# The down-projection of a feed-forward layer in seven products: the sum product moved to third place

## The chip, the cores and the metric

One of the eight cores of a Trainium2 chip runs the kernel. The metric is device time in microseconds (us) from one launch; lower is better. A core has TensorE (PE, matrix multiply, results in PSUM), VectorE (DVE), ScalarE (ACT), GpSimd (POOL) and SyncE (SP, which here issues DMA transfers). PEld is TensorE's loading of the stationary operand.

## The reference

A decoder layer on 1024 tokens of width 1024: a mixing part (pooling and differential attention), then a gated feed-forward part with 2816 channels. The change lies in the last matrix product of it:

```python
    h = rms_norm(x, norm_ffn_g[l], NORM_EPS)
    gu = h @ ffn_w_in[l].astype(h.dtype)
    g = causal_depthwise_conv(gu[..., :D_FF], ffn_conv_w[l], ffn_conv_b[l])
    u = gu[..., D_FF:]
    x = x + (jax.nn.silu(g) * u) @ ffn_w_out[l].astype(h.dtype)
return rms_norm(x, norm_final_g, NORM_EPS)
```

`ffn_w_out` is 2816 x 1024; all data are float32.

## The kernel before

Each float32 operand is split into a rounded high part (ScalarE, L85) and a remainder (L86: `lo = src - hi`, on VectorE or GpSimd); a product is then three matmuls, high by high, high by low and low by high (`mm3`, L148 to L151).

The down-projection (L730 to L864) doesn't compute its four output quarters with eight block products but with seven, in the Strassen-Winograd way. The contraction over 2816 channels is cut into two halves of 11 tiles (channel tiles with even and with odd number), the 1024 output columns into two halves of 512, the tokens into two halves of four tiles. The activations' seven left operands are written to DRAM by the up-projection (`act_d`, rows "1" to "7"; `store_act`, L704; the last sums of them are lines L716 to L719). The weight has four quarters: x (first channel half, first column half), y (first, second), z (second, first) and v (second, second). Each takes three of the 14 buffers of the pool `h2` and comes in six transfers (`load_quarter`, L742). Three of the seven right operands are quarters as loaded, and four are differences, made in place by "updates" on VectorE (L757), in the order in which `DOWN` (L30) names them: x becomes y - x, later x becomes v - x; y becomes v - y; z becomes x - z.

One product runs over six steps (`STEPS`: five of two channel tiles, one of one). For a step, `operands` (L752) issues the update if there is one, loads the activations' rows (`ra`, two buffers) on SyncE's queue, splits them into `ah` (ScalarE) and `al` (VectorE), and splits the weight: high part on ScalarE, remainder on GpSimd. Steps 2, 4 and 6 put the weight's two parts into one `h2` buffer (named `b`), the other three into `bh` and `bl`; buffer tag "st" of `bh` and "sm" of `bl` are also used by sums of the up-projection. `tile_part` (L783) then does the step's matmuls for four token tiles, each into its own PSUM bank (`banks`, L777: products in even places take two "tp" banks, one "mm" and the "pv" bank; those in odd places three "sc" and one "mm"). After its last step a product's banks are added to the residual rows `xr` (`add_product`, L789; one addition of 128 x 512 per token tile and output quarter). `ADDS` (L32) says which quarters: (h, c) is token half h and column half c. Product 1 is wanted in all four quarters and product 6, too, in three of them. Together there are 56 additions (4 of them are the subtractions of product 4, L793).

The order before is 1, 2, 5, 7, 6, 3, 4. After the last product's steps 1 to 3, the final norm of the first four token tiles is done, then steps 4 to 6 and the norm of the others (`held`, `right_half`, `finish`).

The order in which each engine gets its instructions is not that of the code: the framework schedules all of them when the kernel is built, on a timeline of its own, and chooses a free buffer of a tag there. An engine then works its list off in that order and waits at an instruction whose inputs aren't there.

Of the kernel before, what the change touches and what calls it, by code (L numbers as in the profile page):

```python
# [22 lines left out]
NCT = FF // P  # L23
# [3 lines left out]
LAM_INIT = 0.8 - 0.6 * math.exp(-0.3 * 0)  # L27
NEG = -1e30
TW = 384
DOWN = (("1", "x", None), ("2", "z", None), ("5", "x", "yx"), ("7", "y", "vy"), ("6", "x", "vx"), ("3", "v", None),  # L30
        ("4", "z", "xz"))
ADDS = {"1": ((0, 0), (0, 1), (1, 0), (1, 1)), "2": ((0, 0),), "3": ((0, 1),), "4": ((1, 0),), "5": ((0, 1), (1, 1)),  # L32
        "6": ((0, 1), (1, 0), (1, 1)), "7": ((1, 0), (1, 1))}
STEPS = ((0, 2), (2, 2), (4, 2), (6, 2), (8, 2), (10, 1))
SCRATCH = 2048
# [13 lines left out]
def trunk_kernel(ctx, tc, x, norm_mix_g, w_in, pool_w, rows, line, rel_bias, w_out, norm_ffn_g,  # L49
                 ffn_w_in, ffn_w_out, norm_final_g, onehot, out):  # L50
    nc = tc.nc
    x, out, w_in, w_out = x[0], out[0], w_in[0], w_out[0]
# [18 lines left out]
    def sc_ps(name):  # L71
        return ps_a.tile([P, 512], F32, tag="sc", bufs=3, name=name)

    def pv_ps(name):
        return ps_a.tile([P, 512], F32, tag="pv", bufs=1, name=name)

    def tp_ps(name):
        return ps_a.tile([P, 4, P], F32, tag="tp", bufs=2, name=name)

    def mm_ps(name):  # L80
        return ps_a.tile([P, 512], F32, tag="mm", bufs=2, name=name)
# [63 lines left out]
                nc.tensor.transpose(tp[:, k, :], xn[:, (4 * q + k) * P:(4 * q + k + 1) * P], ident)  # L145
            psplit(hi[q][:, :, t * P:(t + 1) * P], lo[q][:, :, t * P:(t + 1) * P], tp)

    def mm3(ps, wh, wl, hh, hl, first, last):  # L148
        nc.tensor.matmul(ps, wh, hh, start=first, stop=False)  # L149
        nc.tensor.matmul(ps, wh, hl, start=False, stop=False)  # L150
        nc.tensor.matmul(ps, wl, hh, start=False, stop=last)  # L151


    nc.scalar.preload_act_table_set("natural_log_exp_and_others")
# [117 lines left out]
    def proj_half(ps, wh, wl, half):  # L272
        cs = slice(half * 512, half * 512 + 512)
        for k in range(KC):
            mm3(ps, wh[:, k, :], wl[:, k, :], hTh[k // 4][:, k % 4, cs], hTl[k // 4][:, k % 4, cs],
                k == 0, k == KC - 1)
# [456 lines left out]
    def load_x1_back():  # L733
        for t in range(NT):
            xt = u_tile(F32, f"xr_{t}")
            nc.vector.tensor_copy(xt[:, 0:1], last_w)
            nc.sync.dma_start(xt, x1_d[t * P:(t + 1) * P, :])
            xr.append(xt)
# [3 lines left out]
    def load_quarter(q):  # L742
        b, cs = dict(x=(0, 0), y=(0, 1), z=(1, 0), v=(1, 1))[q]
        src = ffn_w_out.rearrange("(m b p) c -> b p m c", b=2, p=P)[b][:, :, cs * 512:cs * 512 + 512]
        wq[q] = [h2.tile([P, 4, 512], F32, tag="h2", name=f"w{q}{i}") for i in range(3)]
        for m, n in STEPS:
            nc.sync.dma_start(wq[q][m // 4][:, m % 4:m % 4 + n, :], src[:, m:m + n, :])
# [4 lines left out]
    def operands(gi, m, n):  # L752
        num, q, upd = DOWN[gi]
        if upd:
            a, b = upd
            if q == b:
                nc.vector.tensor_tensor(quarter(b, m, n), quarter(a, m, n), quarter(b, m, n), op=ALU.subtract)  # L757
        raw = mid.tile([P, 2, 512], F32, tag="rw", bufs=2, name=f"ra{num}_{m}")[:, 0:n, :]
        nc.sync.dma_start(raw, op_rows(int(num), m, n))
        if gi == 0:  # L760
            a2 = h2.tile([P, 4, 512], F32R, tag="h2", name=f"a{num}_{m}")
            ah, al = a2[:, 0:n, :], a2[:, 2:2 + n, :]
        else:
            ah = wide.tile([P, 2, 512], F32R, tag="x", bufs=4, name=f"ah{num}_{m}")[:, 0:n, :]
            al = mid.tile([P, 2, 512], F32R, tag="cv", bufs=3, name=f"al{num}_{m}")[:, 0:n, :]
        split(ah, al, raw, nc.vector)
        if m // 2 % 2:
            b2 = h2.tile([P, 4, 512], F32R, tag="h2", name=f"b{num}_{m}")
            wh, wl = b2[:, 0:n, :], b2[:, 2:2 + n, :]
        else:  # L770
            wh = mid.tile([P, 2, 512], F32R, tag="st", bufs=2, name=f"bh{num}_{m}")[:, 0:n, :]
            pool, tag, bufs = (mid, "sm", 2) if gi else (wide, "x", 4)
            wl = pool.tile([P, 2, 512], F32R, tag=tag, bufs=bufs, name=f"bl{num}_{m}")[:, 0:n, :]
        split(wh, wl, quarter(q, m, n))
        return ah, al, wh, wl

    def banks(gi):  # L777
        if gi % 2:
            return [sc_ps(f"fo_{gi}_{j}") for j in range(3)] + [mm_ps(f"fo_{gi}_3")]
        return ([tp_ps(f"fo_{gi}_{j}").rearrange("p a b -> p (a b)") for j in range(2)]  # L780
                + [mm_ps(f"fo_{gi}_2"), pv_ps(f"fo_{gi}_3")])

    def tile_part(ps, op, j, m, n):  # L783
        ah, al, wh, wl = op
        js = slice(j * P, (j + 1) * P)
        for i in range(n):
            mm3(ps, ah[:, i, js], al[:, i, js], wh[:, i, :], wl[:, i, :], m + i == 0, m + i == NCT // 2 - 1)

    def add_product(num, j, ps):  # L789
        for h, c in ADDS[num]:  # L790
            t, cs = 4 * h + j, slice(c * 512, c * 512 + 512)
            if num == "4":
                nc.vector.tensor_tensor(xr[t][:, cs], xr[t][:, cs], ps, op=ALU.subtract)  # L793
            else:
                nc.vector.tensor_tensor(xr[t][:, cs], xr[t][:, cs], ps, op=ALU.add)  # L795
# [3 lines left out]
    def half_sum(t, half):  # L799
        if t not in outs:  # L800
            outs[t] = h2.tile([P, 4, 512], F32, tag="h2", name=f"o_{t}").rearrange("p a c -> p (a c)")[:, 0:D]
            sums[t] = small.tile([P, 2], F32, tag="fs", bufs=8, name=f"ss2_{t}")
        nc.scalar.activation(outs[t][:, 0:512], xr[t][:, half * 512:half * 512 + 512], AF.Square,
                             accum_out=sums[t][:, half:half + 1])

    def finish(t):
        o, ss = outs[t], sums[t]
        var = small.tile([P, 1], F32, tag="var", name=f"varl_{t}")
        nc.vector.tensor_scalar(var, ss[:, 0:1], 1.0 / D, ss[:, 1:2], op0=ALU.mult, op1=ALU.add)
        sd = small.tile([P, 1], F32, tag="lg", name=f"sd_{t}")  # L810
        nc.scalar.activation(sd, var, AF.Sqrt)
        r = small.tile([P, 1], F32, tag="rs", name=f"rsl_{t}")
        nc.vector.reciprocal(r, sd)
        r = newton(r, var, f"l{t}")
        nc.scalar.mul(o[:, 512:1024], o[:, 512:1024], r)
        nc.vector.scalar_tensor_tensor(o[:, 0:512], xr[t][:, 0:512], r, g_bc3[:, 0:512], op0=ALU.mult, op1=ALU.mult)
        if t < NT - 1:
            nc.sync.dma_start(out[t * P:(t + 1) * P, :], o)
            return
        nc.scalar.dma_start(out[t * P:(t + 1) * P, 512:1024], o[:, 512:1024])  # L820
        nc.sync.dma_start(out[t * P:(t + 1) * P, 0:512], o[:, 0:512])

    def right_half(t):
        half_sum(t, 1)
        nc.vector.tensor_scalar(sums[t][:, 1:2], sums[t][:, 1:2], 1.0 / D, EPS, op0=ALU.mult, op1=ALU.add)
        nc.gpsimd.tensor_tensor(outs[t][:, 512:1024], xr[t][:, 512:1024], g_bc3[:, 512:1024], op=ALU.mult)

    last_w = w_now["3"][0][:, 0, 0:1].bitcast(F32)
    late = 3
    for gi, (num, q, upd) in enumerate(DOWN):  # L830
        for c in (q if upd is None else upd):
            if c not in wq:
                load_quarter(c)
        if gi == 4:
            g_bc3 = mid.tile([P, D], F32, tag="gt", bufs=1, name="g_fin")
            nc.sync.dma_start(g_bc3, norm_final_g.unsqueeze(0).to_broadcast((P, D)))
        ps = banks(gi)
        last = gi == len(DOWN) - 1
        held = []
        for si, (m, n) in enumerate(STEPS):  # L840
            op = operands(gi, m, n)
            if last and si >= late:
                held.append((op, m, n))
                continue
            for j in range(4):
                tile_part(ps[j], op, j, m, n)
            if gi == 0 and si == 3:
                load_x1_back()
        if gi == 2:
            warm = small.tile([P, 1], F32, tag="warm", bufs=1, name="warm")  # L850
            nc.scalar.activation(warm, xr[0][:, 0:1], AF.Sqrt, bias=1.0, scale=0.0)
        if last:
            for t in range(NT):
                right_half(t)
            for t in range(4):
                half_sum(t, 0)
                finish(t)
        for j in range(4):
            for op, m, n in held:
                tile_part(ps[j], op, j, m, n)  # L860
            add_product(num, j, ps[j])
            if last:
                half_sum(4 + j, 0)
                finish(4 + j)  # L864
# [55 lines left out]
```

## Time and profile before

| | us |
|---|---|
| median of 3 runs | 1087.63 |
| the 3 runs | 1083.22, 1087.63, 1090.09 |
| profiled execution, its own time | 1088.16 |
| profiled execution, span from first to last instruction | 1086.3 |

The mean granted clock of TensorE in the span is 0.986 of full speed. The profile is one execution. Its times start with the span. Instructions of one engine can overlap a little at their ends, and the ends of matmuls are modelled, so the distance from start to start says what one costs. Idle time of an engine that nothing waits for costs nothing. The down-projection's matmuls begin at 856 us, between the last ones of the up-projection, and end at 1078.8 us. From 864.4 us on there are no others.

### The profile page before, as it was taken

How to read it: one execution, taken by the hardware profiler on the slowest of the kernel's cores; microseconds unless marked ns; L12 is line 12 of the kernel's file. 1: busy time of each engine (PE TensorE's matmuls, PEld its weight loads, DVE VectorE, ACT ScalarE, POOL GpSimd, SP SyncE). 2: the span in 40 equal slices, each digit the busy share in tenths (PEclk: the TensorE clock that was granted, in tenths of full speed). 3: DMA queues.
4: the chain of work that ended last, by engine and by line, in shares of the span. 5: the costliest groups of instructions: out<-in, count | busy, mean ns of one | idle time of the engine just before them, and what ended most of it. 6: DMA issues, size and time to landing. Idle time of an engine off the chain costs nothing. (4 is left out here: it accounts for less than half of the span.)

```text
span 1086.3 us, 13526 instructions
## 1 busy us (share of the span) xinstructions
PE 1034.2 (95%) x4879; PEld 859.7 (79%) x4879; DVE 746.2 (69%) x1192; ACT 513.5 (47%) x827; POOL 452.5 (42%) x304
## 2 busy tenths in 40 slices
PE   5999999999799998899999999999999998999997
PEld 4988888888677776778888888888888887788885
DVE  7556777868587579766775566567555678977646
ACT  5557467665763345434343344334343443345363
POOL 3232232433631235425444362444434455299342
PEclk9999999999899999999999999999999998999999
DMA  7111111101367753232322333232334784533333
GB/s 236 41 39 40 44 28 39 38 27 46 116 214 235 231 193 117 80 95 87 126 90 92 129 108 97 88 126 93 97 120 157 291 284 166 171 113 89 106 107 155
DMA packets 103686, 129.06 MB, mean 119 GB/s; under 512 B 4802, under 2 KB 67487, under 8 KB 103620
## 3 DMA queue, kind: packets, MB, share of 16 engines
q1 hardware_dynamic: 95268, 106.71, 30.8%
q10 hardware_dynamic: 8352, 21.50, 5.1%
q8 instruction: 38, 0.62, 0.2%
q14 instruction: 28, 0.23, 0.1%
HBM read 91.22 MB, written 36.97 MB: 118 GB/s over the span
## 5 line engine op out<-in xcount | busy, mean ns | idle before, releaser
L638 POOL TENSOR_TENSOR sa<-rg 128x512 f32<-128x512 f32 x22 | 32.3, 1470 | 164.7 <-DMA rg<-in_ffn_w_in_dram 124.2
L86 DVE TENSOR_TENSOR al<-ra,ah 128x1024 fp32r<-128x1024 f32 (+1 forms) x36 | 63.6, 1774 | 42.9 <-PE fo L151 22.4
L86 POOL TENSOR_TENSOR ul<-ru,uh 128x1024 fp32r<-128x1024 f32 x22 | 57.3, 2606 | 25.9 <-ACT uh L85 25.4
L372 ACT ACTIVATE p<-p,nm 128x128 f32<-128x128 f32 (+7 forms) x64 | 49.6, 776 | 38.6 <-DVE nm L371 37.7
L85 ACT CAST ah<-ra 128x1024 fp32r<-128x1024 f32 (+1 forms) x36 | 35.1, 977 | 64.4 <-DMA ra<-act_rows 56.5
L359 POOL CAST qz<-q 64x128 fp32r<-64x128 f32 x64 | 22.3, 351 | 96.3 <-PE s L363 88.3
L660 PE MATMUL p<-t4h,gt 128*128 128x512 f32 x176 | 59.1, 397 | 2.0 <-DVE g L685 2.0
L546 PE MATMUL o<-woh,yh 128*128 128x512 f32 x128 | 52.3, 410 | 7.0 <-DVE x L549 4.3
L85 ACT CAST uh<-ru 128x1024 fp32r<-128x1024 f32 x22 | 23.2, 1054 | 72.3 <-PE p L660 66.6
L639 DVE TENSOR_TENSOR sa<-sa,ru 128x512 f32<-128x512 f32 x22 | 39.9, 1812 | 25.3 <-POOL sa L638 25.3
L151 PE MATMUL fo<-bh,al 128*128 128x512 f32 x144 | 56.0, 390 | 0.8 <-DVE al L86 0.8
L149 PE MATMUL fo<-bh,ah 128*128 128x512 f32 x144 | 56.0, 389 | 0.0
L150 PE MATMUL fo<-bl,ah 128*128 128x512 f32 x144 | 56.0, 389 | 0.0
L547 PE MATMUL o<-wol,yh 128*128 128x512 f32 x128 | 51.4, 402 | 2.3 <-POOL wol L86 2.3
L151 PE MATMUL fo<-b,al 128*128 128x512 f32 x120 | 47.9, 404 | 3.5 <-DVE al L86 3.5
L548 PE MATMUL o<-woh,yl 128*128 128x512 f32 x128 | 51.0, 399 | 0.0
L85 ACT CAST gt<-rg 128x512 fp32r<-128x512 f32 x22 | 13.8, 625 | 78.4 <-PE p L660 73.2
L687 DVE TENSOR_TENSOR g<-eb,p 128x512 f32<-128x512 f32 x22 | 15.1, 687 | 49.7 <-PE p L660 49.7
L149 PE MATMUL fo<-b,ah 128*128 128x512 f32 x120 | 47.4, 395 | 0.0
L150 PE MATMUL fo<-b,ah 128*128 128x512 f32 x120 | 47.2, 395 | 0.0
L549 DVE TENSOR_TENSOR x<-x,o 128x512 f32<-128x512 f32 x48 | 32.6, 683 | 20.6 <-PE o L548 19.2
L685 DVE TENSOR_TENSOR g<-eb,p 128x512 f32<-128x512 f32 x22 | 15.0, 681 | 41.1 <-ACT eb L684 41.1
(313 smaller groups left out, 3557.5 us busy)
## 6 DMA issues: line engine op xcount, KB each, us to landing
ra<-act_rows SPq DMA_DIRECT2D x35, 512.0 KB, 3.8
x_rows<-x ACTq DMA_DIRECT2D x24, 512.0 KB, 4.5
ru<-in_ffn_w_in_dram SPq DMA_DIRECT2D x22, 512.0 KB, 4.0
rg<-in_ffn_w_in_dram SPq DMA_DIRECT2D x22, 512.0 KB, 4.1
act_rows<-sm SPq DMA_DIRECT2D x44, 256.0 KB, 2.0
act_rows<-cv ACTq DMA_DIRECT2D x33, 256.0 KB, 2.4
x<-in_x_dram SPq DMA_DIRECT2D x16, 512.0 KB, 5.2
x<-x_rows SPq DMA_DIRECT2D x16, 512.0 KB, 4.6
```

The source lines that it names most:

```text
L85: nc.scalar.copy(hi, src)
L86: (lo_eng or nc.gpsimd).tensor_tensor(lo, src, hi.bitcast(F32), op=ALU.subtract)
L149: nc.tensor.matmul(ps, wh, hh, start=first, stop=False)
L150: nc.tensor.matmul(ps, wh, hl, start=False, stop=False)
L151: nc.tensor.matmul(ps, wl, hh, start=False, stop=last)
L372: nc.scalar.activation(s[:, 0:w], s[:, 0:w], AF.Exp, bias=negm[:, c:c + 1], accum_out=sums[:, c:c + 1])
L546: nc.tensor.matmul(ps, yh[:, ts], wh[:, cs], start=n == 0, stop=False)
L547: nc.tensor.matmul(ps, yh[:, ts], wl[:, cs], start=False, stop=False)
L548: nc.tensor.matmul(ps, yl[:, ts], wh[:, cs], start=False, stop=n == len(wo) - 1)
L549: nc.vector.tensor_tensor(xt[:, cs], xt[:, cs], ps, op=ALU.add)
L639: nc.vector.tensor_tensor(s2, s1, a11, op=ALU.subtract)
L660: nc.tensor.matmul(ps, w[:, k, :], h[:, k, :], start=start and k == 0 and n == 0, stop=k == 3 and n == 2, skip_group_check=not start)
```

## The change

The products come in the order 1, 5, 6, 2, 7, 3, 4. Product 6 has no banks of its own: it goes on summing, without a start flag, into those of product 1 (`ps_all[0]`), so that after it the banks hold the sum of products 1 and 6. Product 1 alone is added only to quarter (0, 0), which product 6 isn't part of; the sum goes to the other three, in `add_product` of product 6. That makes 44 additions. The weight quarters are loaded in the order x, y, v, z instead of x, z, y, v, since a quarter is loaded where a product first wants it. The loading of the final norm's gain stays at the fifth product, and the warming of the Sqrt table on ScalarE (L851) goes from the third to the fifth.

```diff
-DOWN = (("1", "x", None), ("2", "z", None), ("5", "x", "yx"), ("7", "y", "vy"), ("6", "x", "vx"), ("3", "v", None),
+DOWN = (("1", "x", None), ("5", "x", "yx"), ("6", "x", "vx"), ("2", "z", None), ("7", "y", "vy"), ("3", "v", None),
         ("4", "z", "xz"))
-ADDS = {"1": ((0, 0), (0, 1), (1, 0), (1, 1)), "2": ((0, 0),), "3": ((0, 1),), "4": ((1, 0),), "5": ((0, 1), (1, 1)),
+ADDS = {"1": ((0, 0),), "2": ((0, 0),), "3": ((0, 1),), "4": ((1, 0),), "5": ((0, 1), (1, 1)),
         "6": ((0, 1), (1, 0), (1, 1)), "7": ((1, 0), (1, 1))}
...
-    def mm3(ps, wh, wl, hh, hl, first, last):
-        nc.tensor.matmul(ps, wh, hh, start=first, stop=False)
+    def mm3(ps, wh, wl, hh, hl, first, last, more=False):
+        nc.tensor.matmul(ps, wh, hh, start=first, stop=False, skip_group_check=more)
...
-    def tile_part(ps, op, j, m, n):
+    def tile_part(ps, op, j, m, n, more):
...
-            mm3(ps, ah[:, i, js], al[:, i, js], wh[:, i, :], wl[:, i, :], m + i == 0, m + i == NCT // 2 - 1)
+            mm3(ps, ah[:, i, js], al[:, i, js], wh[:, i, :], wl[:, i, :], m + i == 0 and not more,
+                m + i == NCT // 2 - 1, more)
...
+    ps_all = {}
...
-        ps = banks(gi)
+        ps = ps_all[0] if num == "6" else banks(gi)
+        ps_all[gi] = ps
...
-                tile_part(ps[j], op, j, m, n)
+                tile_part(ps[j], op, j, m, n, num == "6")
...
-        if gi == 2:
+        if gi == 4:
             warm = small.tile([P, 1], F32, tag="warm", bufs=1, name="warm")
```

## Rows read from the trace of the kernel before

**Rows 1.** The page: busy time of each engine (share of the span), instructions.

```profile
PE 1034.2 (95%) x4879; PEld 859.7 (79%) x4879; DVE 746.2 (69%) x1192; ACT 513.5 (47%) x827; POOL 452.5 (42%) x304
```

**Rows 2.** Stretches of products 2, 5, 6, 4 and the tail; first line: columns.

```profile
core 0: us, PE busy (x) PEld busy (x) DVE busy (x) ACT busy (x) POOL busy (x), PEclk, DMA share, GB/s
...
891.38:927.64 36.26, 32.79 (x133) 26.59 (x132) 26.42 (x30) 12.43 (x14) 16.57 (x7) 0.91 0.53 188
927.64:958.90 31.26, 30.49 (x133) 24.57 (x132) 29.43 (x27) 10.18 (x11) 13.71 (x4) 1.00 0.45 148
...
988.82:1018.74 29.92, 29.92 (x133) 24.78 (x132) 19.14 (x18) 12.96 (x15) 20.11 (x8) 1.00 0.31 98
...
1048.66:1078.76 30.10, 30.09 (x133) 24.60 (x131) 23.26 (x58) 17.38 (x48) 18.45 (x10) 1.00 0.40 144
1078.76:1086.30 7.54, 0.00 (x0) 0.00 (x0) 3.12 (x8) 2.17 (x5) 0.00 (x0) 0.75 0.40 154
```

**Rows 3.** Timeline, TensorE in product 2: start, us, instruction, [idle before, releaser].

```profile
907.71 0.39 PE L149 MATMUL fo<-b,ah 128*128 128x512 f32 x1
...
909.29 0.39 PE L150 MATMUL fo<-b,ah 128*128 128x512 f32 x1
913.14 0.79 PE L151 MATMUL fo<-b,al 128*128 128x512 f32 x1 [3.47 <-DVE al L86]
...
918.78 0.39 PE L149 MATMUL fo<-b,ah 128*128 128x512 f32 x1
```

**Rows 4.** Timeline, VectorE from 860 to 930 us.

```profile
860.17 0.68 DVE L716 TENSOR_TENSOR sm<-cv 128x512 f32<-128x512 f32 x1
...
877.43 2.61 DVE L717 TENSOR_TENSOR sm<-cv,cv 128x512 f32<-128x512 f32 x1
...
885.60 5.64 DVE L86 TENSOR_TENSOR al<-ra,ah 128x1024 fp32r<-128x1024 f32 x2
892.69 1.23 DVE L86 TENSOR_TENSOR al<-ra,ah 128x1024 fp32r<-128x1024 f32 x1 [1.46 <-ACT ah L85]
896.62 1.23 DVE L757 TENSOR_TENSOR wx<-wy,wx 128x1024 f32<-128x1024 f32 x1 [2.70 <-DMA wy<-in_ffn_w_out_dram]
...
901.29 7.26 DVE L795 TENSOR_TENSOR xr<-xr,fo 128x512 f32<-128x512 f32 x12
908.47 3.49 DVE L757 TENSOR_TENSOR wx<-wy,wx 128x1024 f32<-128x1024 f32 x3
911.87 1.22 DVE L86 TENSOR_TENSOR al<-ra,ah 128x1024 fp32r<-128x1024 f32 x1
```

**Rows 5.** Timeline, SyncE's queue: issues of quarters z and y.

```profile
867.14 1.96 SPq L747 DMA_DIRECT2D wz<-in_ffn_w_out_dram  x4
...
875.63 1.24 SPq L747 DMA_DIRECT2D wz<-in_ffn_w_out_dram  x2
...
891.73 1.97 SPq L747 DMA_DIRECT2D wy<-in_ffn_w_out_dram  x4
```

**Rows 6.** Tile wz: from issue to landing of its six transfers.

```profile
DMA to landing us min/median/max: 6.4/7.5/8.5
```

**Rows 7.** Timeline, GpSimd ahead of product 2.

```profile
879.45 5.67 POOL L86 TENSOR_TENSOR b<-wz,b 128x1024 fp32r<-128x1024 f32 x2
...
886.78 3.38 POOL L86 TENSOR_TENSOR bl<-wz,bh 128x1024 fp32r<-128x1024 f32 x1
```

**Rows 8.** Instructions of single lines and tiles: count, ns min/median/max, first and last start.

```profile
L795 DVE TENSOR_TENSOR xr<-xr,fo x52: 674/680/682, 897.8 to 1049.2; 128x512 f32<-128x512 f32 x52
L86 DVE TENSOR_TENSOR al<-ra,ah x36: 677/1368/3419, 885.6 to 1067.6; 128x1024 fp32r<-128x1024 f32 x30, 128x512 fp32r<-128x512 f32 x6
L757 DVE TENSOR_TENSOR wx<-wy,wx x6: 1218/1219/2864, 896.6 to 913.0; 128x1024 f32<-128x1024 f32 x5, 128x512 f32<-128x512 f32 x1
L757 DVE TENSOR_TENSOR wy<-wv,wy x6: 676/1211/3423, 924.7 to 951.4; 128x1024 f32<-128x1024 f32 x5, 128x512 f32<-128x512 f32 x1
L85 ACT CAST bh<-wz x6: 1039/1046/1053, 882.1 to 1057.5; 128x1024 fp32r<-128x1024 f32 x6
```

More of the change, by code (lines that the diff above doesn't have):

```diff
@@ L146, in to_channels @@
             psplit(hi[q][:, :, t * P:(t + 1) * P], lo[q][:, :, t * P:(t + 1) * P], tp)
-    def mm3(ps, wh, wl, hh, hl, first, last):
-        nc.tensor.matmul(ps, wh, hh, start=first, stop=False)
-        nc.tensor.matmul(ps, wh, hl, start=False, stop=False)
-        nc.tensor.matmul(ps, wl, hh, start=False, stop=last)
+    def mm3(ps, wh, wl, hh, hl, first, last, more=False):
+        nc.tensor.matmul(ps, wh, hh, start=first, stop=False, skip_group_check=more)
+        nc.tensor.matmul(ps, wh, hl, start=False, stop=False, skip_group_check=more)
+        nc.tensor.matmul(ps, wl, hh, start=False, stop=last, skip_group_check=more)
     nc.scalar.preload_act_table_set("natural_log_exp_and_others")
@@ L859, in trunk_kernel @@
             for op, m, n in held:
-                tile_part(ps[j], op, j, m, n)
+                tile_part(ps[j], op, j, m, n, num == "6")
             add_product(num, j, ps[j])
```

## Prediction, made before the changed kernel ran

> **What bounds the kernel now.** I read the page first, then the stretches of the seven down products, then the time lines of TensorE and VectorE where a product runs long, then ScalarE, GpSimd and the SyncE queue around it. On the page TensorE is busy 95% of the span [rows 1], so time can only be won where it stands still or runs slowly. The down-projection is seven products of 132 matmuls (11 channel tiles, 4 token tiles, 3 terms). The stretches [rows 2] show what one costs: product 6 takes 29.92 us from its first matmul to the next product's first one, and so do 7 and 3, whose rows are left out, so 0.227 us for a matmul at granted clock 1.00. Against that, product 2, which stands second, takes 36.26 us: 6.34 too many, at clock 0.91. Product 5, which stands third, takes 31.26 us: 1.34 too many. Product 4 takes 30.10: 0.18 too many. Together 7.86 us. This is all that the stage can give back, 0.72% of the span; the 7.54 us of the tail are made of other work.
>
> Where product 2 loses its 6.34 us: TensorE runs dry in the fourth of its six steps [rows 3]. It waits 3.47 us for a VectorE instruction that writes `al`, the low part of the activations, and goes on with matmuls 0.43 us apart until 918.78, which is the 1.2 GHz level; from there they are 0.23 apart again, at 2.4 GHz. So the wait is 3.47 us and the slow clock behind it the other 6.34 - 3.47 = 2.87.
>
> Why that `al` was late [rows 4]: VectorE finished the `al` before it at 893.9, stood still for 2.70 us until weight quarter y had landed, and then ran, without a pause until 911.87, first updates of x (L757), then the 16 additions of product 1 (L795), then more updates. The `al` that TensorE wanted came behind them, 911.87 to 913.09. The 16 additions and two updates start at 896.62 and are through at 908.47. Twelve additions in a row take 7.26 us, 0.605 each.
>
> **The change, part by part.** *Additions.* Product 1 gives 4 instead of 16 additions, product 6 keeps its 12: 12 fewer, 12 x 0.605 = 7.26 us of VectorE, all just at the place where TensorE ran dry. If all else stood as before, the late `al` would start at 911.87 - 7.26 = 904.61 and end at 905.8. TensorE came to the step that wants it at 907.71 and ran out at 909.68, so the `al` would be there 1.9 us before it is first asked for. The wait and the slow clock behind it go: -6.34 us. Bounds: nothing (another wait at that place) and -6.34.
>
> *Accumulating in PSUM.* Product 6 has the same 132 matmuls; only the start flag is missing. I cost it at nothing; the bounds are 0 and 0, since all products, whatever their start flags, run at 0.227. The four banks of product 1 are held through products 5 and 6, but product 5 takes four others, as product 2 does now, and product 2 follows 30 us after product 5 has left them. The 4 additions that read the banks end about 2.5 us after product 1; product 6 writes there 30 us later.
>
> *Order of the products and the loads.* Now quarter y is loaded second, in z's place. z's six transfers were issued from 867.14 to 876.9 and took 6.4 to 8.5 us to land [rows 5, 6], so y should be in place from about 874, and its last part by 885; v goes where y went (from 891.73), z where v went. The number of transfers on the SyncE queue is unchanged, as are the loads of the activations. v is needed 30 us after its issue, z likewise: covered.
>
> The exposed part is the start of product 5. In second place, it needs for each step an update of x on VectorE (1.22 us [rows 8]), then the rounding on ScalarE (1.04), then the remainder on GpSimd (2.4 to 3.4) before TensorE may start. Product 2 needed only the last two, and had its first step ready just in time: GpSimd began its remainders at 879.45 and ended at 890.16, 10.7 us later [rows 7], 1.22 before TensorE began product 2 at 891.38. That is the margin. At the same time VectorE had to finish the last sums of the activations (L717 to L719), 8.2 us for the three (877.43 to 885.60 [rows 4]), while one of the same kind took 0.68 at 860. Bounds for the new wait at this place: below, 0, if the updates fall into VectorE's idle places before the sums, and because with GpSimd idle the three sums may take 0.68 each and end 6 us sooner. Above: the first update only after the sums (885.6 at the price seen, 881.4 if only the first sum stays slow); from 881.4, 1.22 + 1.04 + the same 10.7 us of remainders make 894.4, so 3.0 us of wait, and one spell of slow clock as measured, 2.87: 5.9 us. I take 1.2: two updates ahead of the sums push all of that by 2.4 us, of which the margin takes 1.22. This is nearer to the lower end because the idle places are there and the sums get cheaper.
>
> *The other updates.* 6 of y and 6 of z are as many as before; before, they were mixed into product 5's stretch, at 1.21 each, and cost 1.34 there. I keep that 1.34 and product 4's 0.18 (bounds 0 and 1.34). The table warm-up moves from the third product to the fifth; on ScalarE it is one small instruction that waits for an addition, and in the stretches where it will stand, ScalarE is busy for less than half the time [rows 2].
>
> *A rule beside this.* The additions took 674 to 682 ns in all 52 cases, also while GpSimd worked; the `al` (two inputs in SBUF) took 677 to 3419 [rows 8]. The Trainium skill, "SBUF — State Buffer", section "Who interferes with whom", says that a VectorE instruction with at most one SBUF input does not contend with GpSimd, and one with two SBUF inputs does. The rows agree. By that rule the change removes the kind that never contends and moves the kind that does, the updates, next to GpSimd's remainders: it speaks against the change, and the third rival below has its result. By the row of the uncontended update the start costs 1.2, by the contended one the third rival's sum.
>
> *Sum.* In the profiled execution: 1086.3 - 6.34 + 1.2 = 1081.2 us of span. The median of the runs, 1087.63, is 1.3 above that span (the profiled execution's own time is 1088.16), so 1082.5.
>
> **The rivals.** (1) *A new wait takes the old one's place*: product 5 starts late at the upper bound, 5.9 us, and pays the slow clock. 1087.63 - 6.34 + 5.9 = 1087.2. For it: the margin of only 1.22 us, and a wait on y's transfer ahead of the sums as the 2.70 us on y now. Against it: y is issued 24 us before it is needed.
>
> (2) *The change doesn't do what it says*: the additions were not what kept the `al`; with 12 fewer, the updates of y, which become ready as soon as v lands, fill their place (6 x 1.21 = 7.26 us, by chance the same sum), and TensorE runs dry as before. 1087.63 + 1.2 = 1088.8 at most. For it: updates did run ahead of `al` in the rows. Against it: the additions come ahead of the `al` in the rows too, and 16 of them took longer than all updates there.
>
> (3) *Slower: VectorE becomes the bound of product 5.* If updates and `al` both meet GpSimd's remainders, a step costs 3.42 (the dearest update) + 2.8 (an `al` at 885.6 to 891.2) = 6.2 us against TensorE's 5.44; six steps and 4 additions make 39.8 in a stretch of 29.9, 9.9 lost, and one spell of slow clock: 12.8. 1087.63 - 6.34 + 12.8 = 1094.1; with the 6 updates of y in the same stretch 6 more, 1100. It decides from the point where update and `al` together pass 4.6 us a step, (29.9 - 2.4) / 6. Against it: GpSimd worked only 16.6 of the 36.3 us of product 2, and updates there took 1.22 as a rule.
>
> **How the numbers follow.** Forecast (1078 to 1085): 0.60. Rivals (1) and (2), about 1087 to 1089: 0.25 together. Rival (3): 0.12. Something else: 0.03. The range runs from 1077.5 (all 7.86 back, 1079.8, less 2 for the scatter of the runs) to 1091, which leaves out the dearer half of rival (3). The forecast's own range is 1078 to 1085. About 1% is what a measurement of this kernel can tell from no change, that is 10.9 us. Faster by more than that would need more than the stage loses at all (7.86): 0.04, for scatter. Slower by more than 1% needs 1098.5, the dear end of rival (3), which I give half of its chance, and something else: 0.08 together. Within 1%: 0.88.
>
> **What would show it right or wrong.** Right: the second product's stretch takes 30 to 32 us at clock 1.00, with no `al` wait of more than 1 us in its fourth step; 4 additions between 891 and 900, 44 in all; matmuls still 0.227 apart in product 6. Rival (1): TensorE idle between products 1 and 5, ahead of it GpSimd's remainder of x, and a stretch of clock below 1. Rival (2): a wait for `al` again, with updates of y ahead of it. Rival (3): VectorE busy throughout product 5 and updates at 2 us or more. A loss in a later product, or any movement before 860 us, would make the sum wrong.

## The result and the profile after

The changed kernel takes 1093.57 us (median of 11 runs, 1090.64 to 1096.10) against 1087.27 for the kernel before in the same series (1083.22 to 1091.68): a ratio of 1.0063, with a 95% interval of 1.0047 to 1.0078. It is slower by about 6.3 us. The forecast was 1082.5, the range 1077.5 to 1091. The profiled execution took 1095.25, with a span of 1093.1 and a mean granted clock of 0.981. Compared with [rows 1], VectorE's instructions fall from 1192 to 1180, by the 12 additions, and its busy time falls by 10 us; TensorE's busy time rises by 2.2 us.

The line of busy times from the page, and the 40 additions (with the 4 subtractions of product 4 that makes 44) from the groups by line:

```profile
PE 1036.4 (95%) x4879; PEld 862.6 (79%) x4879; DVE 736.0 (67%) x1180; ACT 514.2 (47%) x827; POOL 442.7 (40%) x304
...
L796 DVE TENSOR_TENSOR xr<-xr,fo 128x512 f32<-128x512 f32 x40 | 24.6, 682 | 0.0
```

The stretches of products 5, 6, 2, 4 and the tail, with the columns of [rows 2] and to be read against them:

```profile
892.43:935.78 43.35, 35.14 (x133) 27.98 (x132) 34.26 (x26) 13.70 (x15) 22.15 (x9) 0.84 0.45 157
935.78:965.70 29.92, 29.92 (x133) 24.77 (x132) 13.74 (x17) 9.99 (x12) 8.39 (x4) 1.00 0.55 159
965.70:995.62 29.92, 29.92 (x133) 24.77 (x132) 25.54 (x22) 12.69 (x15) 23.98 (x10) 1.00 0.30 97
...
1055.46:1085.57 30.11, 30.08 (x133) 24.59 (x131) 23.25 (x58) 17.40 (x48) 18.43 (x10) 1.00 0.38 144
1085.57:1093.10 7.53, 0.00 (x0) 0.00 (x0) 3.12 (x8) 2.15 (x5) 0.00 (x0) 0.77 0.40 153
```

Products 6, 2, 7 and 3 all run at the 29.92 us of an undisturbed product, product 4 takes what it took before, and so does the tail. Everything that is lost is lost in one place: product 5, now second, takes 43.35 us, 13.43 too many, at clock 0.84. VectorE is busy for 34.26 us of it, with only 26 instructions. TensorE's time line in product 5 shows two stops:

```profile
892.43 0.39 PE L149 MATMUL fo<-bh,ah 128*128 128x512 f32 x1
898.16 0.79 PE L150 MATMUL fo<-bl,ah 128*128 128x512 f32 x1 [5.34 <-POOL bl L86]
...
916.11 0.39 PE L149 MATMUL fo<-b,ah 128*128 128x512 f32 x1
...
919.59 0.79 PE L151 MATMUL fo<-b,al 128*128 128x512 f32 x1 [2.87 <-DVE al L86]
...
925.73 0.42 PE L150 MATMUL fo<-b,ah 128*128 128x512 f32 x1
...
927.62 0.39 PE L149 MATMUL fo<-bh,ah 128*128 128x512 f32 x1
```

Steps 1 to 3 take 916.11 - 892.43 = 23.68 us instead of 3 x 5.44 = 16.32: 7.36 lost, 5.34 of it waiting for GpSimd's remainder and the rest at the slow clock. Step 4 takes 927.62 - 916.11 = 11.51 instead of 5.44: 6.07 lost, 2.87 of it waiting for `al`; then the matmuls run 0.43 apart until 925.73, as they did in [rows 3]. The balance: 7.36 + 6.07 lost now, less the 6.34 that product 2 and the 1.34 that product 5 lost before, makes +5.75. The rest of the 6.8 us between the two spans was there before the products began: one and the same small copy on VectorE starts at 849.88 before and at 850.93 after, 1.05 us later. Product 1's end moves by more than that from one kernel's profile to the next (see the experiments), so this part is taken as scatter.

**The first stop** is a matter of GpSimd's list. Its time line, and ScalarE's casts ahead of it:

```profile
886.57 2.84 POOL L86 TENSOR_TENSOR b<-wx,b 128x1024 fp32r<-128x1024 f32 x1 [2.85 <-ACT b L85]
893.56 1.26 POOL L86 TENSOR_TENSOR b<-wx,b 128x512 fp32r<-128x512 f32 x1 [4.15 <-ACT b L85]
894.78 5.65 POOL L86 TENSOR_TENSOR bl<-wx,bh 128x1024 fp32r<-128x1024 f32 x2
```

```profile
887.35 1.04 ACT L85 CAST bh<-wx 128x1024 fp32r<-128x1024 f32 x1
892.87 0.62 ACT L85 CAST b<-wx 128x512 fp32r<-128x512 f32 x1 [4.48 <-DVE wx L757]
```

The remainder of step 6 (the only one of 128x512) stands in GpSimd's list ahead of that of step 1. Step 1's high part was ready at 888.4, but GpSimd stood still for 4.15 us until step 6's was there, at 893.5; the remainder that TensorE wanted began only at 894.78. Step 6 was late because its update stood on VectorE behind the sums and two `al`, as the last of the pair that starts at 891.02 (below). The order of the list is the old one: before, too, step 6's remainder stood ahead of step 1's (the one at 886.78 in [rows 7]), but as no update was needed, it waited for only 0.16 us:

```profile
885.28 1.54 POOL L86 TENSOR_TENSOR b<-wz,b 128x512 fp32r<-128x512 f32 x1 [0.16 <-ACT b L85]
```

**The second stop** is a matter of VectorE's list. Its time line up to the `al` of step 4:

```profile
891.02 1.81 DVE L757 TENSOR_TENSOR wx<-wy,wx 128x1024 f32<-128x1024 f32 x2
...
898.14 3.37 DVE L757 TENSOR_TENSOR wx<-wv,wx 128x1024 f32<-128x1024 f32 x1 [2.24 <-POOL bl L86]
901.44 1.21 DVE L757 TENSOR_TENSOR wy<-wv,wy 128x1024 f32<-128x1024 f32 x1
...
907.23 2.24 DVE L757 TENSOR_TENSOR wy<-wv,wy 128x1024 f32<-128x1024 f32 x1
909.39 3.41 DVE L757 TENSOR_TENSOR wx<-wv,wx 128x1024 f32<-128x1024 f32 x1
912.73 1.21 DVE L757 TENSOR_TENSOR wy<-wv,wy 128x1024 f32<-128x1024 f32 x1
913.86 1.22 DVE L757 TENSOR_TENSOR wx<-wv,wx 128x1024 f32<-128x1024 f32 x1
915.00 3.41 DVE L757 TENSOR_TENSOR wy<-wv,wy 128x1024 f32<-128x1024 f32 x1
918.33 1.21 DVE L86 TENSOR_TENSOR al<-ra,ah 128x1024 fp32r<-128x1024 f32 x1
```

Before, the same `al` stood behind five updates and 16 additions, 15.25 us from 896.62 to 911.87 [rows 4]. Now it stands behind nine updates (four of x for product 6, five of y for product 7) and four additions, 20.19 us from 898.14 to 918.33. With an update at 1.13 and an addition at 0.60 from start to start that would be 12.6; four of the updates took 2.2 to 3.4 us, and each lies beside a remainder on GpSimd (one of step 3, which ends at 900.43, one of step 5, two of product 6). That makes the other 7.6. The last three of these remainders:

```profile
905.61 2.78 POOL L86 TENSOR_TENSOR b<-wx,b 128x1024 fp32r<-128x1024 f32 x1 [5.17 <-ACT b L85]
908.35 3.37 POOL L86 TENSOR_TENSOR bl<-wx,bh 128x1024 fp32r<-128x1024 f32 x1
913.97 3.35 POOL L86 TENSOR_TENSOR b<-wx,b 128x1024 fp32r<-128x1024 f32 x1 [2.25 <-ACT b L85]
```

### The profile page after: what moved, and what is told of

The parts are those of the page before. It is cut to its first block, busy times and chain, and to the rows that moved or that the text cites. A ratio compares the mean times of both kernels' runs of the same rounds, so it can differ in the third digit from the quotient of the medians.

```text
span 1093.1 us, 13523 instructions
## 1 busy us (share of the span) xinstructions
PE 1036.4 (95%) x4879; PEld 862.6 (79%) x4879; DVE 736.0 (67%) x1180; ACT 514.2 (47%) x827; POOL 442.7 (40%) x304
## 5 line engine op out<-in xcount | busy, mean ns | idle before, releaser
L86 DVE TENSOR_TENSOR al<-ra,ah 128x1024 fp32r<-128x1024 f32 (+1 forms) x36 | 52.1, 1452 | 57.7 <-PE fo L151 49.0
L86 POOL TENSOR_TENSOR ul<-ru,uh 128x1024 fp32r<-128x1024 f32 x22 | 57.3, 2605 | 26.6 <-ACT uh L85 25.9
L687 DVE TENSOR_TENSOR g<-eb,p 128x512 f32<-128x512 f32 x22 | 15.1, 686 | 48.0 <-PE p L660 48.0
L400 DVE SCALAR_TENSOR_TENSOR p<-p,rc,p 128x128 f32<-128x128 f32 (+7 forms) x32 | 32.9, 1031 | 14.9 <-ACT p L399 14.6
```

The costliest lines, as they stand in the source:

```text
L86: (lo_eng or nc.gpsimd).tensor_tensor(lo, src, hi.bitcast(F32), op=ALU.subtract)
L400: nc.vector.scalar_tensor_tensor(s[0][:, 0:w], s[0][:, 0:w], r[:, 0:1], s[1][:, 0:w], op0=ALU.mult, op1=ALU.add)
```

## The experiments

In what follows `tc.issue_after(x)` puts the instructions inside it later than x in the order that the framework builds, and adds no wait of its own on the chip; `ExitStack()` stands for no such rule. Lines left out of a diff are marked by dots; where nothing else is said, it is against the changed kernel. The kernels ran in three series (product 2 second, the y updates later, both edges, the additions later; then 56 additions, no remainders of product 6, the additions first, three edges; then the GpSimd edge alone and y behind product 6), each beside runs of the kernel before, whose medians were 1088.47, 1088.85 and 1088.69. One measure helps to compare their traces, since product 1 ends anywhere from 887.6 to 892.4 us in these executions: the length of the **stage** from the first matmul of the product in second place to the end of the last matmul. It is 187.37 before (891.38 to 1078.75) and 193.11 after (892.43 to 1085.54). Undisturbed it would be 6 x 29.92 = 179.5.

### The change with all 56 additions

```diff
-ADDS = {"1": ((0, 0),), "2": ...
+ADDS = {"1": ((0, 0), (0, 1), (1, 0), (1, 1)), "2": ...
...
-        ps = ps_all[0] if num == "6" else banks(gi)
+        ps = banks(gi)
...
-                tile_part(ps[j], op, j, m, n, num == "6")
+                tile_part(ps[j], op, j, m, n, False)
```

> The order of the changed kernel (1, 5, 6, 2, 7, 3, 4; y loaded second), but product 6 in banks of its own and 56 additions as before: the new order alone. Theory (the order costs two stops, and 12 additions on the way to the fourth step's al are worth their 7.3 us there): the second stop grows by about 7 us, 1099 to 1102. Rival (the additions lie beside other waits and are worth nothing): as the changed kernel, 1093 to 1095.

Measured: 1100.97 us, ratio 1.0115 (1.0095 to 1.0134), stage 201.17. The order without the saving costs about 12 us against the kernel before. The 12 additions are worth 7.4 us by the medians, 8.1 by the stages and 5.8 if each kernel is taken against the kernel before in its own series. VectorE has all 16 additions and seven updates ahead of the `al` of step 4, and y updates again ahead of that of step 5. The expectation had the time right and the place wrong: the stop in step 4 didn't grow (2.22 us), and a new one of 5.48 came in step 5:

```profile
906.89 4.86 DVE L796 TENSOR_TENSOR xr<-xr,fo 128x512 f32<-128x512 f32 x8
...
915.08 1.21 DVE L86 TENSOR_TENSOR al<-ra,ah 128x1024 fp32r<-128x1024 f32 x1
...
919.02 6.22 DVE L757 TENSOR_TENSOR wy<-wv,wy 128x1024 f32<-128x1024 f32 x3
```

```profile
927.57 0.80 PE L151 MATMUL fo<-bh,al 128*128 128x512 f32 x1 [5.48 <-DVE al L86]
```

So the additions' price of 7.26 us in the forecast was about right; it was paid against the new order, not against the old kernel.

### The GpSimd edge alone

```diff
...
-        split(wh, wl, quarter(q, m, n))
+        with tc.issue_after(marks["bl"].ins) if gi == 1 and m == 10 else ExitStack():
+            lo = split(wh, wl, quarter(q, m, n))
+        if gi == 1 and m == 0:
+            marks["bl"] = lo
```

> The changed kernel with one edge of issue order: on GpSimd, the remainder for step 6 of product 5 behind that for step 1. Theory (the start is held up by that one place in GpSimd's list; the second stop depends on VectorE alone and doesn't move): the start's wait falls from 5.3 us to below 1, TensorE reaches the fourth step some 6 us earlier and waits there as much longer for the same al, with one spell of slow clock less: 1089 to 1092. Rival (the two stops are one, the second follows from the first): both shrink, 1086 or less.

Measured: 1091.21 us, ratio 1.0026 (1.0007 to 1.0045). The first stop went and the second grew:

```profile
888.85 0.50 PE L150 MATMUL fo<-bl,ah 128*128 128x512 f32 x1 [0.85 <-POOL bl L86]
...
914.92 0.80 PE L151 MATMUL fo<-b,al 128*128 128x512 f32 x1 [9.23 <-DVE al L86]
```

The stage is 193.16 us, to 0.05 that of the change itself. The `al` of step 4 is ready 27.3 us after the product's first matmul (914.87 - 887.61), and 27.1 in the change (919.54 - 892.43); an undisturbed TensorE asks for it after 16.8. So in the profiled executions VectorE's list sets the stage's length, and the stop at the start only decides where TensorE waits for it. That the two agree to 0.05 us is partly chance: in the change, VectorE stood still for 2.24 us at 898.14, since GpSimd's late remainder still had to read the data; here that wait is gone, but the last two updates for product 5 now meet GpSimd and take 3.99 us instead of 1.81:

```profile
886.48 3.99 DVE L759 TENSOR_TENSOR wx<-wy,wx 128x1024 f32<-128x1024 f32 x2
```

The median lies 2.4 us lower than the change's all the same (2.5 above the kernel before in its own series, against 6.3); the profiled stage has no place for that, and it stays open.

### The updates of y later

```diff
...
-                nc.vector.tensor_tensor(quarter(b, m, n), quarter(a, m, n), quarter(b, m, n), op=ALU.subtract)
+                with tc.issue_after(marks["al5"].ins) if num == "7" else ExitStack():
+                    nc.vector.tensor_tensor(quarter(b, m, n), quarter(a, m, n), quarter(b, m, n), op=ALU.subtract)
...
-        split(ah, al, raw, nc.vector)
+        marks["al"] = split(ah, al, raw, nc.vector)
+        if gi == 1 and m == 10:
+            marks["al5"] = marks["al"]
```

> The changed kernel, with the six updates of y (wanted by the fifth product) issued on VectorE only behind the last al of product 5. Theory (two separate stops in product 5; the second one is the fourth step's al behind ten updates in VectorE's list): the stop in the fourth step goes, 6.1 us, the one at the start (7.4 us) stays: 1087.5 (1086 to 1089). Rival (VectorE simply has too much to do there, and whatever is put back is missing elsewhere): the wait turns up again in products 5 or 6, 1092 to 1095.

Measured: 1087.84 us, ratio 0.9975 (0.9956 to 0.9994), stage 188.15. The `al` of step 4 starts at 906.93, 16.8 us after the product's first matmul, and of the two stops only the one at the start is left; the six y updates run later, from 917.21, with GpSimd idle until 922.74:

```profile
896.10 0.80 PE L150 MATMUL fo<-bl,ah 128*128 128x512 f32 x1 [5.54 <-POOL bl L86]
```

```profile
906.93 1.21 DVE L86 TENSOR_TENSOR al<-ra,ah 128x1024 fp32r<-128x1024 f32 x1
...
917.21 6.36 DVE L760 TENSOR_TENSOR wy<-wv,wy 128x1024 f32<-128x1024 f32 x6
```

The change costs nothing any more against the kernel before. So with the updates for product 7 out of the way of that `al` the loss is gone; product 7 begins only at 995.62 in the profile of the change, with products 6 and 2 in between.

### No remainders of product 6's weight

This kernel leaves out the remainders of product 6's weight: GpSimd writes zeros instead, so that it no longer reads the weight. VectorE's list stays as it is.

```diff
-        split(wh, wl, quarter(q, m, n))
+        if num == "6":
+            nc.scalar.copy(wh, quarter(q, m, n))
+            nc.gpsimd.memset(wl.bitcast(F32), 0.0)
+        else:
+            split(wh, wl, quarter(q, m, n))
```

> The changed kernel without the remainders of product 6's weight: GpSimd fills them with zeros instead of reading x and the high part (so part of product 6 is left out), and no longer reads x beside VectorE's updates there. Theory (of the ten updates ahead of the fourth step's al in product 5 about half took 3.4 us instead of 1.2 because GpSimd's remainders ran at the same time; remainders of product 6 were two of the four): those updates fall to 1.2, the al comes 4 us earlier, the second stop goes, the first stays: 1087 to 1089. Rival (the price of the updates isn't GpSimd's doing): the dear updates stay and the time is 1093 to 1095.

Measured: 1088.28 us, ratio 0.9990 (0.9979 to 1.0001), stage 187.06. The stop at the start is the same (5.37), the second is gone. The updates that had taken 2.2 and 3.4 us take 1.21, except the first one, beside step 3's remainder, and one beside that of step 5 (GpSimd, 907.29 to 910.50):

```profile
907.03 1.21 DVE L757 TENSOR_TENSOR wy<-wv,wy 128x1024 f32<-128x1024 f32 x1
908.17 3.41 DVE L757 TENSOR_TENSOR wx<-wv,wx 128x1024 f32<-128x1024 f32 x1
...
913.78 1.21 DVE L757 TENSOR_TENSOR wy<-wv,wy 128x1024 f32<-128x1024 f32 x1
914.91 1.21 DVE L86 TENSOR_TENSOR al<-ra,ah 128x1024 fp32r<-128x1024 f32 x1
```

So the same list without this contention is through 3.2 us earlier, reckoned from the product's first matmul (22.7 instead of 25.9), and that, too, is enough: the y updates and the contention made the second stop together, and without either it is gone. It is the behaviour that the forecast cited from the Trainium skill, "SBUF — State Buffer", section "Who interferes with whom"; the trace agrees: 1.21 alone, 3.4 beside a GpSimd subtraction.

### The kernel before, with its 16 additions later

This edit is against the kernel before.

```diff
...
+            if gi == 1 and si == 3:
+                with tc.issue_after(marks["al"].ins):
+                    for j in range(4):
+                        add_product("1", j, ps_1[j])
...
-            add_product(num, j, ps[j])
+            if gi:
+                add_product(num, j, ps[j])
```

> The kernel before, with its order of products and all 56 additions, the 16 additions of product 1 issued on VectorE behind the al of product 2's fourth step. Theory (it is what stands ahead of the al in the list, not the number of additions): product 2 loses at most 2 us instead of 6.3, 1081 to 1083. Rival (12 additions fewer are needed; put later, they only make the fifth step's al late): 1086 to 1088.

Measured: 1092.58 us, ratio 1.0030 (1.0008 to 1.0051), stage 192.49. A miss: the order of the additions was thought to be enough. The wait of step 4 falls from 3.47 to 1.82, and step 5 has one of 4.21 behind the 16 additions, as the expectation's rival had it. More telling is what stands ahead of the `al` of step 4:

```profile
896.09 10.18 DVE L759 TENSOR_TENSOR wx<-wy,wx 128x1024 f32<-128x1024 f32 x5 [2.77 <-DMA wy<-in_ffn_w_out_dram]
906.19 3.40 DVE L86 TENSOR_TENSOR al<-ra,ah 128x1024 fp32r<-128x1024 f32 x1
909.51 9.64 DVE L797 TENSOR_TENSOR xr<-xr,fo 128x512 f32<-128x512 f32 x16
```

The five updates that had taken about 5.65 us among the additions (15.25 less 16 x 0.6) now take 10.18. Where additions had run beside GpSimd's remainders (902.6 to 907.4 before), updates and an `al` run now (remainders from 901.9 to 911.9). Taking an addition away from such a place moves into it an instruction that does contend.

### Product 2 left in second place, sum in PSUM

```diff
-DOWN = (("1", "x", None), ("5", "x", "yx"), ("6", "x", "vx"), ("2", "z", None), ("7", "y", "vy"), ...
+DOWN = (("1", "x", None), ("2", "z", None), ("5", "x", "yx"), ("6", "x", "vx"), ("7", "y", "vy"), ...
-        if gi % 2:
+        if gi in (1, 2, 4, 6):
```

> Sum of products 1 and 6 in PSUM and 44 additions as in the changed kernel, but z stays second: order 1, 2, 5, 6, 7, 3, 4, weight quarters loaded x, z, y, v as before. Theory (the first term of the prediction, taken alone, is right, and the loss comes from product 5 in second place): the 12 additions that stood ahead of the fourth step's al in product 2 are gone, al ends near 906 us, product 2 takes 30 to 31 us instead of 36.3, time 1081 (1080 to 1083). Rival (the additions never kept the al; updates or the later transfers do): product 2 still waits in its fourth step, 1086 to 1088. Second rival (products 2 and 5 now share four banks, so product 5 waits for product 2's additions): a stop of 2 us or more at the start of product 5, 1084 or more.

Measured: 1092.86 us, ratio 1.0041 (1.0018 to 1.0064), stage 194.85. This has the saved additions without the new order ahead of product 2. The wait of step 4 falls from 3.47 to 0.91 (and 0.41 in step 5): the forecast's first term holds here in kind. But the expectation's second rival came true: while product 1's banks wait for product 6, product 5 has to take the banks that product 2 has just used, and the four additions that free them stand behind updates which wait for v:

```profile
934.41 0.76 PE L149 MATMUL fo<-bh,ah 128*128 128x512 f32 x1 [10.37 <-DVE xr L796]
```

```profile
924.62 1.23 DVE L757 TENSOR_TENSOR wx<-wv,wx 128x1024 f32<-128x1024 f32 x1 [2.68 <-DMA wv<-in_ffn_w_out_dram]
...
933.60 1.87 DVE L796 TENSOR_TENSOR xr<-xr,fo 128x512 f32<-128x512 f32 x3
```

### The same, with product 2's additions ahead of the updates

This edit is against the kernel of the section before this one.

```diff
...
-                nc.vector.tensor_tensor(quarter(b, m, n), quarter(a, m, n), quarter(b, m, n), op=ALU.subtract)
+                with tc.issue_after(marks["add2"].ins) if gi > 2 else ExitStack():
+                    nc.vector.tensor_tensor(quarter(b, m, n), quarter(a, m, n), quarter(b, m, n), op=ALU.subtract)
...
-                nc.vector.tensor_tensor(xr[t][:, cs], xr[t][:, cs], ps, op=ALU.add)
+                marks["add" + num] = nc.vector.tensor_tensor(xr[t][:, cs], xr[t][:, cs], ps, op=ALU.add)
```

> As e2 (z second, order 1, 2, 5, 6, 7, 3, 4, sum of products 1 and 6 in PSUM, 44 additions), with all later updates (of x for product 6, of y and of z) issued on VectorE behind the additions of product 2. Theory (in e2 product 5 waited 10.4 us for banks, because product 2's four additions stood behind five updates that waited for quarter v): the wait at the start of product 5 falls below 2 us, the rest stays as in e2, 1082 to 1085. Rival (sharing the banks costs this whatever stands ahead): 1090 or more. Second rival (the updates put back are missing later): a new al wait or remainder wait in products 5 or 6, 1086 to 1089.

Measured: 1090.22 us, ratio 1.0009 (0.9993 to 1.0024), stage 189.91. A miss in the time. The wait for banks falls from 10.37 to 1.99, and the last step of product 5 gets a wait for `al` of 2.77 at 957.74, behind the updates that were put back, again beside GpSimd: a stop removed and the next one made, as the second rival had it, but dearer.

### Both edges: GpSimd's order and the updates of y

The edits of the GpSimd edge and of the later y updates together.

> The changed kernel with two changes of issue order alone: the updates of y behind the last al of product 5 on VectorE, and on GpSimd the remainder for step 6 of product 5 behind that for step 1. Theory (both stops come from the order of the lists that the build made): both go, 13.4 us of product 5's 43.4, 1080 to 1083. Rival (product 5 in second place lacks time on VectorE or GpSimd whatever the order): a start that is still 3 us late or more, or another al wait, 1086 or more.

Measured: 1088.67 us, ratio 0.9994 (0.9976 to 1.0011), stage 188.55. A miss. The two old stops go (0.76 is left at the start), and two others appear, one in step 5 and one at the start of product 6:

```profile
917.18 0.50 PE L151 MATMUL fo<-bh,al 128*128 128x512 f32 x1 [2.49 <-DVE al L86]
...
928.55 0.50 PE L150 MATMUL fo<-bl,ah 128*128 128x512 f32 x1 [3.14 <-POOL bl L86]
```

The first comes from a VectorE update of x for product 6 that overwrites the data of step 5 and stood still 2.29 us until GpSimd had read them, ahead of the `al`.

### Three edges: the last x updates later, too

This edit is against the kernel with both edges.

```diff
-                with tc.issue_after(marks["al5"].ins) if num == "7" else ExitStack():
+                late_up = num == "7" or (num == "6" and m >= 8)
+                with tc.issue_after(marks["al5"].ins) if late_up else ExitStack():
```

> As e5, and the last two updates of x for product 6 (steps 5 and 6) issued on VectorE behind the last al of product 5, too. In e5, one of them waited 2.3 us for GpSimd ahead of the al of step 5, TensorE waited 2.5 us for that al and then 3.1 us for a remainder of product 6 that had come late through it. Theory (a chain that starts at this one place in the list): both waits go, 1081 to 1084. Rival (VectorE is at its limit in product 5): another wait of 2 us or more in products 5 or 6, 1086 or more.

Measured: 1089.35 us, ratio 1.0015 (0.9999 to 1.0032), stage 188.33. A miss of the same kind. Product 5 is clean, and product 6's first `al` comes behind the six y updates, which now run beside GpSimd's remainders and take 11.80 us instead of 6.36:

```profile
915.63 11.80 DVE L761 TENSOR_TENSOR wy<-wv,wy 128x1024 f32<-128x1024 f32 x6
927.36 2.35 DVE L86 TENSOR_TENSOR al<-ra,ah 128x1024 fp32r<-128x1024 f32 x2
```

TensorE waited 5.80 us for it.

### The updates of y behind product 6

This edit is against the kernel with three edges.

```diff
-                late_up = num == "7" or (num == "6" and m >= 8)
+                late_up = "al6" if num == "7" else "al5" if num == "6" and m >= 8 else ""
-                with tc.issue_after(marks["al5"].ins) if late_up else ExitStack():
+                with tc.issue_after(marks[late_up].ins) if late_up else ExitStack():
...
+        if gi == 2 and m == 10:
+            marks["al6"] = marks["al"]
```

> As e9, but the six updates of y (wanted by the fifth product alone) are issued on VectorE behind the last al of product 6, not behind that of product 5. In e9 they stood ahead of product 6's first al, took 11.8 us beside GpSimd's remainders, and TensorE waited 5.8 us. Theory (the work that the new order needs early fits into products 5 and 6 once nothing that is wanted later stands ahead of it): no stop above 1.5 us is left, product 5 takes 30 to 32 us and product 6 30, time 1080 to 1083, faster than both kernels. Rival (VectorE's work of this stretch doesn't fit whatever the order): another stop of 2 us or more, 1086 or more.

Measured: 1084.25 us (12 runs, 1080.30 to 1088.10), ratio 0.9959 (0.9939 to 0.9980), stage 183.55, span 1080.4. Time and largest stop lie a little outside the expectation (1080 to 1083, no stop above 1.5 us). All stops that are left on TensorE:

```profile
890.32 0.50 PE L150 MATMUL fo<-bl,ah 128*128 128x512 f32 x1 [0.66 <-POOL bl L86]
...
952.68 0.50 PE L151 MATMUL fo<-bh,al 128*128 128x512 f32 x1 [1.92 <-DVE al L86]
...
975.05 0.50 PE L151 MATMUL fo<-bh,al 128*128 128x512 f32 x1 [0.22 <-DVE al L86]
```

The `al` of steps 4 to 6 come right behind four x updates:

```profile
901.24 4.12 DVE L761 TENSOR_TENSOR wx<-wv,wx 128x1024 f32<-128x1024 f32 x2
905.28 7.36 DVE L86 TENSOR_TENSOR al<-ra,ah 128x1024 fp32r<-128x1024 f32 x3
```

This keeps the whole change and three rules on the order of lists. It beats both kernels, the one before by 0.4% and the change by about 1%. Its span is close to the forecast's 1081.2, but partly by luck, since product 1 ends 2.1 us earlier here than in the profile before; the median is 1.8 us above the forecast's, and the stage 1.3 us longer than the 182.2 that the forecast amounts to (187.37 - 6.34 + 1.2). What the three rules would give without the 12 saved additions was not run.

## Why the prediction was wrong

**What bounds the kernel: right.** TensorE is busy 95% of the span in both, every larger loss is a stop of TensorE or the slow clock behind one, and an undisturbed product takes 29.92. The stage before loses 7.86 us and the change 13.6.

**Additions, -6.34: the step that failed.** The forecast took the 12 additions off VectorE's old list "if all else stood as before". It didn't. The forecast asked of v's earlier load only whether v comes in time ("covered"), not what it sets free. With v's transfers issued from 891.6 to 897.3, before from 919.7 to 943.4, six updates of x and six of y become ready just there, and VectorE works its list off in order. The loss that was gone from product 2 came back in product 5's fourth step: 6.07 against 6.34. This is the second rival's mechanism, at its place and nearly at its price; what it said of the y updates is shown by moving them alone (1087.84); loading v at its old time was not tried. It erred in one thing, that the additions were not what kept the `al`: 12 of them cost some 6 to 8 us in this order, and with product 2 second the wait fell to 0.91 + 0.41. Both were: VectorE's list was long enough to be late with either.

**The start of product 5, +1.2: sized wrong, and above its own upper bound.** The first rival's wait was there, 7.36 us with its slow clock against a bound of 5.9. The bound took the first update to come late and then the old 10.7 us of remainders without a pause. In fact the updates began early (875.74), ahead of the sums, as the lower bound had it, but GpSimd paused for 2.85 and 4.15 us: each remainder now waits for an update and a cast of its own. Step 6 stood ahead of step 1 in GpSimd's list before, too, and its remainder is part of the 10.7; what the bound left out is that step 1's remainder then hangs on the last of the six updates and not on the first. The edge on GpSimd alone shows, however, that this term did not set the stage's length in the profile: without it, the `al` of step 4 took its place to 0.05 us.

**Contention, the third rival: the mechanism held, not its place.** VectorE was not the bound of all steps of product 5, which the rival needed, but four contended updates in a row of nine made 7.6 us of the lateness, and without product 6's remainders the second stop is gone. The forecast wrote that the rule "speaks against the change" and gave it 0.12; the rule was worth more, since it didn't need a whole product, only the list ahead of one `al`. That the rival's 1094.1 lies next to the measured 1093.57 is luck: its sum has contention in all six steps and no stop at the start.

**The other updates, 1.34 kept: wrong, but small.** The products behind product 5 run clean, so the 1.34 was gained. **PSUM at nothing: right**; product 6 takes 29.92 on the banks of product 1. The price of held banks shows where another product has to share the other set: 10.37 us with product 2 second.

**The sum.** Forecast span 1081.2, measured 1093.1, 11.9 apart: 6.07 for the fourth step, 7.36 - 1.2 = 6.16 for the start, less 1.34, and 1.05 that was there before the products. Of the signs named ahead, the 44 additions, 0.227 in product 6, the idle start, the `al` with y updates ahead of it and updates at 2 us or more were all to be seen; the stretch of 30 to 32 us was not, and the four additions of product 1 came between 902.6 and 907.3, not between 891 and 900.

**The range.** Three rivals that can happen at once were priced one by one, each against a forecast in which the others didn't happen. The first and the second did together, with the third inside the second: 1081.2 + 6.16 + 6.07 = 1093.4 of span, outside a range whose upper end came from part of the third alone.

## What to carry to other kernels

A step that is moved forward brings forward the readiness of everything that hangs on its loads: list, engine by engine, what becomes ready at the freed place and stands ahead of the next instruction that the bounding engine waits for, urgent or not. Time freed on an engine that works in order goes to whatever its list holds next, so price a removal together with the new list, or hold the unurgent work back by an explicit order. One such rule tends to move the stop to the next consumer (five kernels here show it); the gain came only once all of the engine's unurgent work was behind the last urgent one.

## What the runs showed of the hardware

A 128x1024 update on VectorE took 1.21 us alone and 3.4 beside a GpSimd subtraction; six in a row took 6.36 with GpSimd idle for nearly all of it and 11.80 beside it, and five took about 5.65 among additions and 10.18 without them. How little of it is enough was not expected: with two of the four meetings gone, the change was no longer slower than the kernel before (1088.28, ratio 0.9990).

The 3.4 us are no fixed price. In the profile of the change, each of the four dear updates ended 1.08 to 1.09 us after the GpSimd subtraction that had begun before it (898.14 + 3.37 = 901.51 against 900.43; 909.47 against 908.39; 912.80 against 911.72; 918.41 against 917.32), and cost 2.2 or 3.4 by how much of the subtraction was left. Where VectorE began first, GpSimd paid: the update at 913.86 took its 1.22, and the subtraction that began at 913.97 took 3.35, against 2.4 alone. In these cases the later of the two behaves as if it waited for the end of the other. A row of VectorE instructions can hold GpSimd up for longer: in the profile before, one subtraction took 8.17 us from 950.26 on, while the updates and `al` from 949.14 to 956.17 kept to 1.21 and 0.68.

Not every stop brought the slow clock. Behind stops of 2.22 and 2.49 us the matmuls went on 0.23 apart, at granted clock 1.00 over the next 4.8 us in the second case; behind 2.77, 2.87 and 5.34 they were 0.43 apart at once, and behind those of 1.99 us (product 2's additions first) and 3.14 us they were 0.23 apart at first and 0.43 from 1.3 and 1.4 us on. So the length of the stop alone doesn't tell. What TensorE did before these stops differs; the runs don't settle what decides.
